# A gated gMLP and Mamba-2 layer on one core: the wide products gathered in three PSUM banks, and sums moved between GpSimd, VectorE and ScalarE

## The chip, the core and the metric

The kernel runs on one core of a Trainium2 chip: TensorE (PE) multiplies 128x128 tiles into PSUM, which has eight banks of 128x512 float32; VectorE (DVE), ScalarE (ACT) and GpSimd (POOL) do the elementwise work; DMA queues are fed by SyncE (SP) and ScalarE. Each engine takes its instructions in a fixed order. The metric is the time of one execution in microseconds (us), lower is better.

## The reference

One layer on a sequence of 1024 positions and 1024 channels, all in float32. Cut to what matters:

```python
h = rms_norm(x, norm_w) * (1 + scale) + shift                 # modulated by c
gm_u, gm_v, gm_z, ssm_z, xbc, dt_raw, g_a, g_b = split(h @ w_in)
y_a = gelu(gm_u) * (W_s @ layer_norm(gelu(gm_v)) + b_s) * silu(gm_z)     # chunks of 128
xs, bm, cm = split(silu(causal_conv(xbc, 4 taps)))
y_b = rms_norm((ssd_scan(xs, softplus(dt_raw), a, bm, cm) + xs * d_skip) * silu(ssm_z))
merged = sigmoid(g_a) * (y_a @ w_proj_a) + sigmoid(g_b) * (y_b @ w_proj_b)
return rms_norm(x + gate * (merged @ w_out))
```

`w_in` has 11296 columns. The product `h @ w_in` is most of the work.

## The kernel before

Float32 accuracy comes from splitting each operand into a high and a low part (`float32r`) and adding three products, high by high, high by low, low by high. Large products also go through a scheme of seven half-size products in place of eight (p1 to p7): sums of the quarters of both operands are taken first, and sums of the seven products afterwards.

**Start** (to about 77 us): norm and modulation of `x`, its sums `b11`, `t1` to `t4`, `b21`, `b22` and their splits, and the columns of `dt` and the first two gates in three accumulators of two banks each.

**Wide stage**: the other columns of `w_in` in 43 pairs of 128 columns (`todo`): four pairs of `gm_v` (`v0` to `v6`), eight that join a block of u and one of z (`uz`), sixteen for the convolution (`cb`, `x`), eight of `ssm_z` (`z`), seven of gates (`g`). For each pair:

- `pair_weights` loads four 128x512 pieces of `w_in` on SP's queue into a ring of eight slots (four pieces and three sums a pair, so the next pair's later pieces wait until slots come free), takes four sums of them (lines 526 to 529, on GpSimd; on VectorE for the first pair), and splits seven operands: a ScalarE copy for the high part (line 489), a VectorE subtraction for the low one (line 490). It is called one pair ahead; the split operands lie in rings of eight.
- `pair` runs the seven products (`product`, line 537, twelve matmuls each) and empties their banks. It takes five of the eight PSUM banks, `a b e c d`, in the order p1(a) p6(b) p7(e) p5(c) p4(d) p2(a again) p3(c again). `a` is copied by ScalarE (lines 550, 573); five sums from PSUM are VectorE's (lines 554, 560, 564, 568, 576). Both halves of an output row, `c1` and `c2`, build on each other in SBUF. An emptying has high priority in the scheduler that fixes each engine's order.
- What follows a pair (`d1`, `d2`): gelu and transposition for v; the convolution, one ScalarE pass, three VectorE passes (line 830) and a silu (line 832) per 128 channels; tanh for gates; for `uz`, sigmoid and products (lines 812 to 820). `mix_load` brings the block's LayerNorm input `vm` back and applies mean and scale in eight VectorE passes of 128 columns (line 791); `mix` multiplies it.
- `later` hangs tasks on slots, one a product: the mix, the weights of `w_proj_b` brought into split form quarter by quarter (`wb_quarter`, lines 735 to 755, from pair 22 on), `w_out` times the gate on GpSimd (line 718).

**After it**: the scan over chunks (two groups of heads in turn; `front`, `back`, `prep`, with the product by `w_proj_a` drawn in between by `draw`), then the product by `w_proj_b` and the one by `w_out`. The scan takes its PSUM tiles from the same eight banks through `bank`.

## Time and profile before

| | |
|---|---|
| median of 3 runs (lowest, highest) | 1453.49 us (1453.35, 1453.54) |
| the profiled execution: time, span, mean clock of TensorE | 1452.97 us, 1451.2 us, 0.993 |
| busy: PE, DVE, ACT, POOL | 97%, 78%, 49%, 33% of the span |

The time of an execution is a little over the span from first to last instruction in its trace. A row of a timeline has start, duration, engine, line, operation, output <- inputs, and in brackets the idle time of the engine before it with what ended it. A row of the waits has who waited for whom, then total, number and longest in us. A row of a group has its number of instructions after x, then busy time and the mean duration of one in ns. Line numbers in rows are those of the kernel they come from.

### The profile page before, as it was taken

The page shows a single profiled execution, that of the slowest core. Times are in us where ns is not written, and L with a number is a line of the kernel's source. Part 1 is how long each engine was busy: PE and PEld are TensorE (multiplying, and loading weights), DVE is VectorE, ACT ScalarE, POOL GpSimd, SP SyncE. Part 2 cuts the span into 40 slices and gives each one's busy share as a digit, 9 for nine tenths or more (in the row PEclk, how much of TensorE's full clock was granted, in tenths as well). Part 3 has the DMA queues.
Part 4 walks back from the last instruction along what each step waited for, and adds up shares of the span by engine and source line. Part 5 has one row for each costly group of instructions (what it writes and reads, how often), then busy time and mean ns, then how long its engine had stood idle before and what let it go on. Part 6 is the DMA issues. An engine that isn't in the chain of part 4 may idle for free.

```text
span 1451.2 us, 20751 instructions
## 1 busy us (share of the span) xinstructions
PE 1405.2 (97%) x7095; PEld 1158.3 (80%) x7095; DVE 1131.7 (78%) x1793; ACT 707.0 (49%) x1284; POOL 480.3 (33%) x366
## 2 busy tenths in 40 slices
PE   8989999999999999899989999999999999999997
PEld 6768888888888788778877888888878878787886
DVE  4676599999999998798999988588777667948443
ACT  5654454544445454444536544478776624334211
POOL 0032124233333233323342433147878840000000
PEclk9999999999999999999999999999999999999999
DMA  8543333323333564778657685598887767977331
GB/s 270 151 129 102 117 95 116 108 83 93 102 117 116 149 190 148 235 215 252 203 168 236 213 263 174 163 314 304 314 291 243 262 199 272 369 250 283 134 116 73
DMA packets 260461, 276.82 MB, mean 191 GB/s; under 512 B 13596, under 2 KB 210628, under 8 KB 260356
## 3 DMA queue, kind: packets, MB, share of 16 engines
q1 hardware_dynamic: 179364, 195.24, 42.6%
q10 hardware_dynamic: 80992, 80.26, 16.6%
q8 instruction: 56, 0.92, 0.3%
q14 instruction: 49, 0.40, 0.1%
HBM read 191.27 MB, written 84.18 MB: 190 GB/s over the span
## 4 chain that ended last, share of the span: by engine, by line
PE 33%; DMA 6%; DVE 5%; issue 3%; POOL 3%; ACT 2%; SPq 1%; POOLq 0%; ACTq 0%; DVEq 0%
PE po L76 6%; PE yp L1386 3%; PE x L1386 3%; PE pma L76 2%; DMA yn<-yb_d 2%; PE cz L537 2%; PE cg L537 1%; PE az L537 1%; PE ag L537 1%; PE yi L76 1%; PE yn L76 1%; DMA dcy<-acs_d 1%; DMA wol<-wo_d 1%; PE sp L76 1%; PE ccb L537 1%
## 5 line engine op out<-in xcount | busy, mean ns | idle before, releaser
L1582 POOL TENSOR_TENSOR r<-r,fnw 128x256 f32<-128x256 f32 (+1 forms) x3 | 2.7, 915 | 253.6 <-ACT xr L1581 253.6
L923 ACT ACTIVATE dcy<-dcy,nacs 128x128 f32<-128x128 f32 x256 | 78.2, 388 | 14.0 <-POOL dcy L918 13.9
L526 POOL TENSOR_TENSOR s1uz<-a21uz,a22uz 128x512 f32<-128x512 f32 x8 | 10.5, 1307 | 143.7 <-DMA a22uz<-in_w_in_dram 107.5
L918 POOL TENSOR_SCALAR_AFFINE_SELECT dcy<-dcy 128x1024 f32<-128x1024 f32 x32 | 35.4, 1108 | 41.7 <-ACT ea L915 41.6
L915 ACT ACTIVATE ea<-dcy 64x512 f32<-64x512 f32 x64 | 40.1, 626 | 17.3 <-DMA dcy<-acs_d 13.1
L832 ACT ACTIVATE ac<-ac 128x1024 f32<-128x1024 f32 x32 | 34.0, 1062 | 26.1 <-DVE ac L830 26.0
L830 DVE SCALAR_TENSOR_TENSOR ac<-c2cb,cwt,ac 128x1023 f32<-128x1023 f32 (+2 forms) x24 | 44.2, 1843 | 0.5 <-issue 0.2
L943 DVE TENSOR_TENSOR dcy<-dcy,pc 128x1024 f32<-128x1024 f32 x32 | 38.9, 1215 | 6.8 <-PE pc L79 5.1
L76 PE MATMUL pma<-yh,wah 128*128 128x512 f32 x128 | 43.4, 419 | 0.1
L971 POOL TENSOR_TENSOR st<-st,cd 128x256 f32<-128x256 f32 x48 | 34.5, 721 | 26.9 <-DVE st L969 16.6
L76 PE MATMUL pma<-yh,wal 128*128 128x512 f32 x128 | 42.7, 415 | 0.0
L1005 POOL TENSOR_TENSOR yz<-y,sl 128x512 f32<-128x512 f32 x32 | 42.3, 1322 | 0.9
L1004 POOL TENSOR_TENSOR y<-y,ym 128x512 f32<-128x512 f32 (+1 forms) x32 | 37.0, 1157 | 13.8 <-DVE ym L1003 13.2
L830 DVE SCALAR_TENSOR_TENSOR ac<-c2x,cwt,ac 128x1023 f32<-128x1023 f32 (+2 forms) x24 | 40.2, 1677 | 1.5 <-ACT ac L828 1.3
L1591 DVE TENSOR_TENSOR r<-po,xr 128x1024 f32<-128x1024 f32 x7 | 8.6, 1225 | 41.1 <-PE po L76 41.1
L791 DVE TENSOR_SCALAR vm<-vm,mv,vr 128x128 f32<-128x128 f32 x64 | 40.6, 704 | 0.0
L1592 ACT ACTIVATE xr<-r 128x1024 f32<-128x1024 f32 x7 | 7.4, 1061 | 67.3 <-issue 39.7
L1003 DVE TENSOR_TENSOR ym<-yn,ea 128x512 f32<-128x512 f32 (+1 forms) x32 | 19.9, 621 | 26.0 <-PE yn L76 25.9
L76 PE MATMUL pma<-yl,wah 128*128 128x512 f32 x128 | 40.1, 394 | 0.0
L526 POOL TENSOR_TENSOR s1x<-a21x,a22x 128x512 f32<-128x512 f32 x8 | 12.3, 1535 | 75.8 <-DMA a22x<-in_w_in_dram 19.3
L76 PEld LDWEIGHTS yn<-sl,st 128*128 128x128 f32 x224 | 30.7, 193 | 8.2 <-issue 2.4
L76 PE MATMUL yn<-sl,st 128*128 128x128 f32 x224 | 32.0, 279 | 4.7 <-DVE st L973 4.0
(2812 smaller groups left out, 4708.2 us busy)
## 6 DMA issues: line engine op xcount, KB each, us to landing
sl<-s_d SPq DMA_DIRECT2D x32, 768.0 KB, 6.1
s_d<-ac ACTq DMA_DIRECT2D x32, 512.0 KB, 3.2
dcy<-acs_d SPq DMA_DIRECT2D x32, 512.0 KB, 8.5
aw<-in_ada_w_dram SPq DMA_DIRECT2D x16, 512.0 KB, 3.9
wbr<-in_w_proj_b_dram SPq DMA_DIRECT2D x64, 128.0 KB, 3.9
wb_d<-wbb ACTq DMA_DIRECT2D x32, 256.0 KB, 3.4
wb_d<-wbc ACTq DMA_DIRECT2D x32, 256.0 KB, 3.2
yb_d<-yz ACTq DMA_DIRECT2D x32, 256.0 KB, 6.1
```

The costliest lines, as they stand in the source:

```text
L76: pin(PE.matmul(acc, l, r, start=first, stop=last))
L537: pin(PE.matmul(ps, lw[:, k * P : (k + 1) * P], r[k], start=first and n + k == 0, stop=n == 2 and k == 3, skip_group_check=not first))
L791: V.tensor_scalar(vn[:, cs], vn[:, cs], mv[:, ch, 0:1], vr[:, 1, ch : ch + 1], op0=ALU.subtract, op1=ALU.mult)
L830: V.scalar_tensor_tensor(ac[:, s:], cc[:, : S - s], conv_wt[:, 3 - s, i : i + 1], ac[:, s:], op0=ALU.mult, op1=ALU.add)
L915: A.activation(ea[hh * HD : (hh + 1) * HD], dcy.rearrange("p (j e) i l -> p e j (i l)", e=2)[hh * HD : (hh + 1) * HD, hh], AF.Exp)
L918: G.affine_select(out=d8, in_=d8, compare_op=ALU.is_ge, fill=-1e30, base=0, pattern=[[0, 2 * HPG], [1, P]], channel_multiplier=-1)
L923: A.activation(dcy[:, h, i, :], dcy[:, h, i, :], AF.Exp, bias=sub[:, i, h : h + 1])
L943: V.tensor_tensor(d3, d3, pc[:, 0:256].unsqueeze(1).to_broadcast([P, HPG, 256]), op=ALU.mult)
L971: G.tensor_mul(v3(s2), v3(self.st), fac(cd, g, s)[:, i].unsqueeze(2).to_broadcast([P, HPG, HD]))
L1004: G.tensor_add(y1[:, :, t0:], y1[:, :, t0:], m[:, :, t0:])
L1005: G.tensor_mul(yz, y1, sl[:, 4:6])
L1386: pin(PE.matmul(ps[j], a[:, v, js], r, start=first and n + k == 0, stop=n == 2 and k == KT - 1, skip_group_check=not first))
```

## The change

Seven products with other banks and in another order; four weight sums and one product from GpSimd to VectorE; the LayerNorm factor from VectorE to ScalarE; sigmoid as one silu on ScalarE; another order of the last pairs.

TensorE. A pair has three banks: x (its own ring of two) gathers p1, then p6, p7 and p4 on top; y gathers p5 and p3; z has p2. x is read out after each product without being cleared. p4 runs in the next pair, after its p5, except where a pair is `whole` (pairs `v6`, `z7` and the last), which ends with p7, p2, p4. One row for each product (four matmuls have it alike but for the tile of k; the rest is left out), in the pair `cb2` before:

```order
L537 MATMUL acb_3121<-b11h_155,p1cb2h 128x512
...
L537 MATMUL bcb_3122<-t2h_163,p6cb2h 128x512
...
L537 MATMUL ecb_3123<-t3h_171,p7cb2h 128x512
...
L537 MATMUL ccb_3124<-t1h_179,p5cb2h 128x512
...
L537 MATMUL dcb_3125<-t4h_187,p4cb2h 128x512
...
L537 MATMUL acb_3121<-b21h_195,p2cb2h 128x512
...
L537 MATMUL ccb_3124<-b22h_203,p3cb2h 128x512
```

and now, with the first products of the pair `uz4`:

```order
L560 MATMUL xcb_3086<-b11h_155,p1cb2h 128x512
...
L560 MATMUL ycb_3101<-t1h_163,p5cb2h 128x512
...
L560 MATMUL xcb_3086<-t2h_171,p6cb2h 128x512
...
L560 MATMUL ycb_3101<-b22h_179,p3cb2h 128x512
...
L560 MATMUL zcb_3158<-b21h_195,p2cb2h 128x512
...
L560 MATMUL xcb_3086<-t3h_187,p7cb2h 128x512
...
L560 MATMUL xuz_3236<-b11h_155,p1uz4h 128x512
...
L560 MATMUL yuz_3264<-t1h_163,p5uz4h 128x512
...
L560 MATMUL xcb_3086<-t4h_203,p4cb2h 128x512
```

Between two products of one bank there are now two others.

ScalarE, at the end of the pair `uz3` and the start of `cb2` (`c1uz` holds the block's u before and its z now, `tz` the tanh for its sigmoid, `p1uz4h` a high part for the pair after), before:

```order
L812 ACTIVATE tz_3035<-c2uz_2995 128x1024
L489 CAST p3cb2h<-s4cb_2917 128x512
L573 COPY c1uz_2980<-auz_2950 128x512
L489 CAST p1uz4h<-a11uz_3078 128x512
L819 ACT_TABLE_LOAD
L819 ACTIVATE c1uz_2980<-c1uz_2980 128x1024
L550 COPY c1cb_3138<-acb_3121 128x512
```

and now:

```order
L576 COPY c1uz_2940<-xuz_2914 128x512
L840 ACTIVATE vm_3031<-vm_3031,vr 128x128 x8
L508 CAST p2cb2h<-a12cb_2877 128x512
L878 ACTIVATE ac_2970<-ac_2970 128x1024
L508 CAST p7cb2h<-a21cb_2873 128x512
L88 DMA s_d_118<-ac_2970 512x1x256
L859 ACTIVATE c1uz_2940<-c1uz_2940 128x1024
L508 CAST p4cb2h<-a22cb_2875 128x512
L508 CAST p1uz4h<-a11uz_3043 128x512
L576 COPY c1cb_3099<-xcb_3086 128x512
```

The eight passes of the LayerNorm factor came in; the first copy of `cb2` no longer has the gelu with its table load just ahead of it.

VectorE at the same place, before:

```order
L814 SCALAR_TENSOR_TENSOR ya_2967<-c2uz_2995,ya_2967 128x1024
L791 TENSOR_SCALAR vm_3064<-vm_3064,mv,vr 128x128 x8
L576 TENSOR_TENSOR c1uz_2980<-c1uz_2980,cuz_2953 128x512
L490 TENSOR_TENSOR p1uz4l<-a11uz_3078,p1uz4h 128x512
L490 TENSOR_TENSOR p6uz4l<-s2uz_3087,p6uz4h 128x512
L554 TENSOR_TENSOR c1cb_3138<-c1cb_3138,bcb_3122 128x512
```

and now, from the p7 addition of the pair `x1` to the p3 addition of `uz3` (two splits and one convolution pass are left out):

```order
L576 TENSOR_TENSOR c2x_2869<-p5x_2792,xx_2764 128x512
L509 TENSOR_TENSOR p4uz3l<-a22uz_2725,p4uz3h 128x512
L876 SCALAR_TENSOR_TENSOR ac_2850<-c1x_2777,cwt,ac_2850 128x1022
...
L876 SCALAR_TENSOR_TENSOR ac_2850<-c1x_2777,cwt,ac_2850 128x1021
L851 SCALAR_TENSOR_TENSOR ya_2927<-mix_0_2928,par_140,bsb 128x512
L851 SCALAR_TENSOR_TENSOR ya_2927<-mix_1_2934,par_140,bsb 128x512
L509 TENSOR_TENSOR p5cb2l<-s1cb_2879,p5cb2h 128x512
L509 TENSOR_TENSOR p6cb2l<-s2cb_2880,p6cb2h 128x512
L876 SCALAR_TENSOR_TENSOR ac_2970<-c2x_2869,cwt,ac_2970 128x1023
...
L876 SCALAR_TENSOR_TENSOR ac_2970<-c2x_2869,cwt,ac_2970 128x1021
L576 TENSOR_TENSOR c1uz_2940<-c1uz_2940,yuz_2942 128x512
```

The factor's block is gone from VectorE. The diff, cut to its core:

```diff
     hpool = tc.tile_pool(name="hpool", bufs=1, reuse_waits="tile")
     hp = hpool.__enter__()
-    BN = ("b11", "t2", "t3", "t1", "t4", "b21", "b22")
+    BN = ("b11", "t1", "t2", "b22", "t3", "b21", "t4")
...
-            pin(A.activation(sg[:, h * 512 : (h + 1) * 512], accs[i][h], AF.Tanh, scale=0.5))
-        store(th_d[(i - 1) * P : i * P, :], sg)
+            A.activation(sg[:, h * 512 : (h + 1) * 512], accs[i][h], AF.Tanh, scale=0.5)
+        later(1 + i, store, th_d[(i - 1) * P : i * P, :], sg)
     def first_dt():
         dtt = wide("dtt")[0:NH, :]
         for h in range(2):
             pin(V.tensor_copy(dtt[:, h * 512 : (h + 1) * 512], accs[0][h][0:NH, :]))
-        store(dt_d, dtt)
+        later(2, store, dt_d, dtt)
...
     def bank(name):
-        return psum.tile([P, 512], F32, name=name, tag="bk", bufs=8)
+        if pairs_done:
+            pairs_done.append(name)
+            if len(pairs_done) % 4 == 2:
+                return psum.tile([P, 512], F32, name=name, tag="px", bufs=2)
+        return psum.tile([P, 512], F32, name=name, tag="bk", bufs=6)
...
-    def split(name, t, keep):
-        hi, lo = wt(f"{name}h", "wh", 8), wt(f"{name}l", "wl", 8)
-        keep(A.copy(hi, t))
-        keep(V.tensor_sub(lo, t, f32(hi)))
-        return hi, lo
-    def pair_weights(name, c1, c2, pinned=False):
+    def pair_weights(name, c1, c2, pinned=False, parts_later=False):
...
         s1, s2, s4 = (wt(f"s{i}{name}", "ws", 8, F32) for i in (1, 2, 4))
         s3 = a["21"]
-        parts = {"p1": a["11"], "p6": s2, "p7": s3, "p5": s1, "p4": a["22"], "p2": a["12"], "p3": s4}
+        parts = {"p1": a["11"], "p5": s1, "p6": s2, "p3": s4, "p2": a["12"], "p7": s3, "p4": a["22"]}
         ops = {}
         def parts_of(*nms):
             for nm in nms:
-                ops[nm] = split(f"{nm}{name}", parts[nm], pin if pinned else lambda i: i)
+                if nm not in ops:
+                    ops[nm] = wt(f"{nm}{name}h", "wh", 8), wt(f"{nm}{name}l", "wl", 8)
+                (hi, lo), t, keep = ops[nm], parts[nm], pin if pinned or parts_later else lambda i: i
+                keep(A.copy(hi, t))
+                keep(V.tensor_sub(lo, t, f32(hi)))
         if pinned:
+            for nm in parts:
+                ops[nm] = wt(f"{nm}{name}h", "wh", 8), wt(f"{nm}{name}l", "wl", 8)
+            parts_of("p1")
+            pin(V.tensor_add(s1, s3, a["22"]))
+            first_dt()
+            parts_of("p5")
+            pin(V.tensor_sub(s2, s1, a["11"]))
+            last_split("t2")
+            parts_of("p6")
+            first_gate(1)
+            first_gate(2)
+            def stage(n):
+                if n == 0:
+                    pin(V.tensor_sub(s4, a["12"], s2))
+                    parts_of("p3")
+                elif n == 1:
+                    parts_of("p2")
+                    pin(V.tensor_sub(s3, a["11"], s3))
+                    last_split("t3")
+                elif n == 2:
+                    parts_of("p7")
+                    last_split("t4")
+                    parts_of("p4")
+                    seconds.extend(pair_weights(*todo[1][:3], parts_later=True))
+                elif n == 3:
+                    seconds[1]("p1")
+                elif n == 4:
+                    seconds[1]("p5", "p6")
+                elif n == 5:
+                    seconds[1]("p3", "p2", "p7", "p4")
+            ops["after"] = stage
+        else:
             V.tensor_add(s1, s3, a["22"])
             V.tensor_sub(s2, s1, a["11"])
...
-        else:
-            G.tensor_add(s1, s3, a["22"])
-            G.tensor_sub(s2, s1, a["11"])
-            G.tensor_sub(s3, a["11"], s3)
-            G.tensor_sub(s4, a["12"], s2)
-            parts_of("p1", "p6", "p7", "p5", "p4", "p2", "p3")
+            V.tensor_sub(s4, a["12"], s2)
+            V.tensor_sub(s3, a["11"], s3)
+            if parts_later:
+                return ops, parts_of
+            parts_of("p1", "p5", "p6", "p3", "p2", "p7", "p4")
         return ops
...
-    def pair(name, ops, done2, done1, after=None):
-        keep = pin if after else lambda i: i
+    pending, pairs_done = [], []
+    def pair(name, ops, done1, done2, after=None, whole=False):
+        keep = pin if name in first_c1 and not p2r else lambda i: i
         after = after or (lambda n: None)
-        pa, pb, pe, pc, pd = (bank(f"{n}{name}") for n in "abecd")
-        product(pa, ops["p1"], "b11")
-        c1 = wide(f"c1{name}")
-        u2 = c1[:, 512:1024]
-        with tc.high_priority():
-            keep(A.copy(u2, pa))
+        def out(f, *a):
+            with tc.high_priority():
+                keep(f(*a))
+        def p2():
+            pz = bank(f"z{name}")
+            product(pz, ops["p2"], "b21")
+            out(V.tensor_add, c1[:, 0:512], c1[:, 0:512], pz)
+        px = psum.tile([P, 512], F32, name=f"x{name}", tag="px", bufs=2)
+        product(px, ops["p1"], "b11")
+        c1 = first_c1.pop(name) if name in first_c1 else wide(f"c1{name}")
+        out(A.copy, c1[:, 0:512], px)
         after(0)
-        product(pb, ops["p6"], "t2")
-        with tc.high_priority():
-            keep(V.tensor_add(u2, u2, pb))
+        py = bank(f"y{name}")
+        product(py, ops["p5"], "t1")
+        c2 = wide(f"c2{name}") if p2r else None
+        p5 = c2[:, 512:1024] if p2r else gm.tile([P, 512], F32, name=f"p5{name}", tag="p5")
+        out(A.copy, p5, py)
         after(1)
-        c2 = wide(f"c2{name}")
-        product(pe, ops["p7"], "t3")
-        u3 = c2[:, 0:512]
-        with tc.high_priority():
-            keep(V.tensor_add(u3, u2, pe))
+        if pending:
+            pending.pop()()
+        product(px, ops["p6"], "t2", False)
+        out(A.copy, c1[:, 512:1024], px)
         after(2)
-        product(pc, ops["p5"], "t1")
-        with tc.high_priority():
-            keep(V.tensor_add(c2[:, 512:1024], u3, pc))
+        product(py, ops["p3"], "b22", False)
+        out(V.tensor_add, c1[:, 512:1024], c1[:, 512:1024], py)
         after(3)
-        product(pd, ops["p4"], "t4")
-        with tc.high_priority():
-            keep(V.tensor_add(u3, u3, pd))
-        after(4)
-        done2(c2)
-        product(pa, ops["p2"], "b21", False)
-        with tc.high_priority():
-            keep(A.copy(c1[:, 0:512], pa))
-        product(pc, ops["p3"], "b22", False)
-        with tc.high_priority():
-            keep(V.tensor_add(u2, u2, pc))
-        done1(c1)
+        if not whole:
+            p2()
+            after(4)
+            done1(c1)
+        product(px, ops["p7"], "t3", False)
+        c2 = c2 or wide(f"c2{name}")
+        out(V.tensor_add, c2[:, 512:1024], p5, px)
+        after(4 if whole else 5)
+        if whole:
+            p2()
+            done1(c1)
+        def p4():
+            product(px, ops["p4"], "t4", False)
+            out(A.copy, c2[:, 0:512], px)
+            done2(c2)
+        if whole:
+            p4()
+        else:
+            pending.append(p4)
...
-    wst = gx.tile([P, NG, P], F32, name="wst", tag="wst")
+    first_c1 = {"v0": gx.tile([P, S], F32, name="c1v0", tag="wst")}
+    wst = None
...
         rsqrt(vr[:, 1, :], vr[:, 0, :], vr[:, 2, :])
+        V.scalar_tensor_tensor(vr[:, 2, :], mv[:, :, 0], -1.0, vr[:, 1, :], op0=ALU.mult, op1=ALU.mult)
...
-            V.tensor_scalar(vn[:, cs], vn[:, cs], mv[:, ch, 0:1], vr[:, 1, ch : ch + 1],
-                            op0=ALU.subtract, op1=ALU.mult)
+            A.activation(vn[:, cs], vn[:, cs], AF.Identity, scale=vr[:, 1, ch : ch + 1], bias=vr[:, 2, ch : ch + 1])
...
     def zg_done(g):
         def done(cz):
-            th = wide(f"tz{g}")
-            A.activation(th, cz, AF.Tanh, scale=0.5)
-            V.scalar_tensor_tensor(cz, th, 1.0, cz, op0=ALU.add, op1=ALU.mult)
-            V.scalar_tensor_tensor(vns[g], cz, 0.5, vns[g], op0=ALU.mult, op1=ALU.mult)
+            A.activation(cz, cz, AF.Silu)
+            V.tensor_mul(vns[g], cz, vns[g])
         return done
     def u_done(g):
         def done(cu):
             A.activation(cu, cu, AF.Gelu_apprx_tanh)
-            G.tensor_mul(cu, cu, vns[g])
+            V.tensor_mul(cu, cu, vns[g])
...
-        jobs.append((f"uz{g}", COL_U + g * P, COL_ZG + g * P, u_done(g), zg_done(g), g))
+        jobs.append((f"uz{g}", COL_ZG + g * P, COL_U + g * P, zg_done(g), u_done(g), g))
     light = [p for q in zip(light, gpairs[:5] + [None] * 3) for p in q if p]
-    n_l = len(light)
-    while convs or light:
-        if convs:
-            jobs.append(convs.pop(0))
-        take = 2 if len(light) > len(convs) else 1
-        for _ in range(take if convs or len(light) < 3 else len(light)):
-            if light:
-                jobs.append(light.pop(0))
+    while convs:
+        jobs.append(convs.pop(0))
+        for _ in range(1 if len(convs) in (1, 4, 7) else 2):
+            jobs.append(light.pop(0))
...
-            later(3, decays, n + 1)
+            later(3 + 5 * n, decays, n + 1)
             g, s = order[n]
-            later(12 + n, groups[g].prep, s)
+            later(13 + n, groups[g].prep, s)
...
-    held = []
-    NPRE = 22
+    held, seconds = [], []
+    NPRE = 20
...
-                later(2 + 4 * i, wb_quarter, i)
+                later(2 + 43 * i // 10, wb_quarter, i)
...
-        if n + 1 < len(todo):
+            first_c1[name] = wide(f"c1{name}")
+        if 0 < n < len(todo) - 1:
             nxt = pair_weights(*todo[n + 1][:3])
...
-            later(1, mix, g)
+            later(1 if g else 3, mix, g)
             if g + 1 < NG:
                 later(7, mix_load, g + 1)
         if n + 1 == len(todo):
-            pair(name, ops, lambda t: held.append((d2, t)), lambda t: held.append((d1, t)), beside)
+            pair(name, ops, lambda t: held.append((d1, t)), lambda t: held.append((d2, t)), beside, True)
         else:
-            pair(name, ops, d2, d1)
-        ops = nxt
+            pair(name, ops, d1, d2, ops.get("after"), n in (3, len(jobs) - 1))
+        ops = nxt if n else seconds[0]
...
+    pairs_done.append("")
...
+    draw(6)
     for n in range(2):
         step(n, "front")
         draw(10)
```

More of the change, by code (lines that the diff above doesn't have):

```diff
@@ L633, in dt_part1d @@
         V.tensor_scalar_mul(dthq, dth, 2.0)
-        later(4, dt_part2, dth, adt)
+        later(8, dt_part2, dth, adt)
     def dt_part2(dth, adt):
@@ L669, in mix_weights2 @@
     def mix_weights2(wsn):
+        nonlocal wst
+        wst = gx.tile([P, NG, P], F32, name="wst", tag="wst")
         for q in range(2):
```

13 lines of the change are left out of this document (removed).

## Prediction

> **What bounds the kernel now.** I read the engine shares first, then the table by stage, then TensorE's waits, then the timelines around the longest of them.
>
> ```profile
> PE 1405.2 (97%) x7095; PEld 1158.3 (80%) x7095; DVE 1131.7 (78%) x1793; ACT 707.0 (49%) x1284; POOL 480.3 (33%) x366
> ...
> 77.00:490.00 413.00, 406.48 (x1879) 336.62 (x1878) 350.63 (x496) 196.21 (x279) 140.33 (x91) 1.00 0.36 110
> 490.00:800.00 310.00, 296.30 (x1287) 241.68 (x1286) 278.20 (x413) 151.10 (x257) 108.41 (x66) 0.98 0.68 203
> 800.00:956.00 156.00, 156.00 (x700) 129.40 (x698) 122.32 (x172) 80.98 (x141) 48.59 (x32) 1.00 0.68 213
> ```
>
> The columns of the lower rows are the stretch and its length, then busy time of TensorE, its weight loads, VectorE, ScalarE and GpSimd, then the clock. The wide stage is 77 to 956 us, 43 column pairs; then comes the scan. TensorE sets the time, so only its idle time and a lowered clock can be won. VectorE is its only rival: 350.63+278.20+122.32 = 751 of the wide stage's 879 us.
>
> ```profile
> PE cz L537 <- DVE c2z L564: 8.0, 4, 3.5
> PE cg L537 <- DVE c2g L564: 5.2, 2, 4.3
> PE cv L537 <- DVE c2v L564: 4.8, 1, 4.8
> ...
> PE cuz L537 <- DVE c2uz L564: 1.7, 1, 1.7
> ...
> PE cx L537 <- DVE c2x L564: 0.5, 1, 0.5
> ```
>
> All waits of the wide products have one form: p3 wants bank `c` again, two products after p5 left it (p4 and p2 lie between), and VectorE has not yet made the addition of line 564 that empties it. They sum to 8.0+5.2+4.8+1.7+0.5 = **20.2 us**. The three longest also lower the clock:
>
> ```profile
> 99.33 2.08 PE L537 MATMUL cv<-b22h,p3v0h 128*128 128x512 f32 x4 [4.77 <-DVE c2v L564]
> ...
> 103.49 1.07 PE L537 MATMUL av<-b11h,p1v2h 128*128 128x512 f32 x4
> ...
> 732.07 2.08 PE L537 MATMUL cg<-b22h,p3g8h 128*128 128x512 f32 x4 [4.30 <-DVE c2g L564]
> 737.22 1.09 PE L537 MATMUL acb<-b11h,p1cb6h 128*128 128x512 f32 x4
> 739.97 1.07 PE L537 MATMUL bcb<-t2h,p6cb6h 128*128 128x512 f32 x4
> 742.69 1.07 PE L537 MATMUL ecb<-t3h,p7cb6h 128*128 128x512 f32 x4
> ...
> 778.10 2.08 PE L537 MATMUL cz<-b22h,p3z4h 128*128 128x512 f32 x4 [3.51 <-DVE c2z L564]
> 782.48 1.08 PE L537 MATMUL ag<-b11h,p1g10h 128*128 128x512 f32 x4
> ```
>
> An undisturbed product of twelve matmuls takes 742.69-739.97 = 2.72 us. After the three waits it took 103.49-99.33 = 4.16, 737.22-732.07 = 5.15 and 782.48-778.10 = 4.38: 1.44+2.43+1.66 = **5.5 us** more. So 25.7 us of the wide stage hang on VectorE being late.
>
> **Why VectorE is late.** Two things, both touched by the change.
>
> ```profile
> 89.41 1.79 DVE L490 TENSOR_TENSOR p2v0l<-a12v,p2v0h 128x512 fp32r<-128x512 f32 x1
> ...
> 96.20 0.67 DVE L554 TENSOR_TENSOR c1v<-c1v,bv 128x512 f32<-128x512 f32 x1
> 96.79 0.68 DVE L490 TENSOR_TENSOR p7v2l<-a21v,p7v2h 128x512 fp32r<-128x512 f32 x1
> ```
>
> ```profile
> 90.72 1.63 POOL L527 TENSOR_TENSOR s2v<-s1v,a11v 128x512 f32<-128x512 f32 x1
> ```
>
> While GpSimd sums weights, VectorE's subtraction of two SBUF tiles takes 1.79 us; alone 0.68. Undisturbed operations of this size follow each other at 0.60 (96.20 to 96.79). An addition out of PSUM keeps 0.67. Over the wide stage the split's subtractions (line 490), the convolution (830) and the LayerNorm factor (791) hold VectorE this long:
>
> ```profile
> 77.00:956.00 879.00, 260.71 (x301) 0.99 0.53 161
> 77.00:956.00 879.00, 145.26 (x96) 0.99 0.53 161
> 77.00:956.00 879.00, 40.56 (x64) 0.99 0.53 161
> ```
>
> 301 at 0.60 would be 181, so 80 us of the first are GpSimd's doing; the convolution's are 1.27 us when undisturbed (row `c1cb` below), 96 x 1.2 = 115 from start to start, so 30 of the second. And a block in the queue makes others late:
>
> ```profile
> 330.02 6.18 DVE L791 TENSOR_SCALAR vm<-vm,mv,vr 128x128 f32<-128x128 f32 x8
> 332.07 1.07 PE L537 MATMUL acb<-b11h,p1cb2l 128*128 128x512 f32 x4
> 336.12 0.68 DVE L576 TENSOR_TENSOR c1uz<-c1uz,cuz 128x512 f32<-128x512 f32 x1
> 336.88 1.28 ACT L819 ACT_TABLE_LOAD   x1 [6.71 <-DVE c1uz L576]
> 339.14 0.57 ACT L550 COPY c1cb<-acb 128x512 f32<-128x512 f32 x1
> ```
>
> Product p1 of `cb2` ended at 333.1; ScalarE copied it 6.0 us later, because it stood behind a gelu that waited for VectorE, which was 6.18 us in line 791.
>
> **The change, part by part.** TensorE's products are as many and as long as before (the same matmuls in another order), so nothing there.
>
> VectorE loses two PSUM additions a pair (86 x 0.60 = 52 us), line 791 (41 us), and the 110 us of GpSimd's disturbance; gains four weight sums in 42 pairs (168 x 0.60 = 101 us) and the product with u. The gates are priced by
>
> ```profile
> L830 DVE SCALAR_TENSOR_TENSOR ac<-c1cb,cwt,ac 128x1023 f32<-128x1023 f32 x8 | 10.2, 1272 | 0.2 <-ACT ac L828 0.2
> L814 DVE SCALAR_TENSOR_TENSOR ya<-c2uz,ya 128x1024 f32<-128x1024 f32 x8 | 10.8, 1354 | 0.0
> L813 DVE SCALAR_TENSOR_TENSOR c2uz<-tz,c2uz 128x1024 f32<-128x1024 f32 x8 | 9.8, 1225 | 3.8 <-ACT tz L812 3.7
> L923 ACT ACTIVATE dcy<-dcy,nacs 128x128 f32<-128x128 f32 x16 | 4.9, 389 | 2.4 <-POOL dcy L918 2.4
> ```
>
> two passes before (9.8+10.8), two multiplications after (16 x 1.2): nothing. Sum: 751-52-41-110+101-1 = 648 us, 76% of a stage of some 855. GpSimd keeps eight multiplications of `w_out`; if each disturbs two operations by 1.79-0.68, the bound from above is 666. ScalarE gains 86 copies at 0.57 and 64 factors; I price these by the nearest row, line 923, 0.39: 428+49+25 = 502 us, 59%. Neither engine is a bound on average.
>
> The banks. Each pair now holds x (p1, p6, p7, p4), y (p5, p3) and z (p2), and every bank is wanted again after two products: 2 x 2.72 = **5.44 us** for an evacuation, where before only `c` had so little. The copy of `acb` above, done 6.6 us after its product, would miss that. What made it late goes: in the new order there stand between ScalarE's copy of p6 in the pair before and this copy the factor's eight passes, two Silus and four casts. With
>
> ```profile
> L832 ACT ACTIVATE ac<-ac 128x1024 f32<-128x1024 f32 x32 | 34.0, 1062 | 26.1 <-DVE ac L830 26.0
> L489 ACT CAST p3cb0h<-s4cb 128x512 fp32r<-128x512 f32 x1 | 0.6, 627 | 0.1
> ```
>
> that is 8 x 0.39+2 x 1.06+4 x 0.63 = 7.8 us of work in the time of four products, 10.9 us. On VectorE, from the p7 addition of a conv pair to the p3 addition of the next stand five operations of 0.60, five of the convolution at 1.2 and two of the mix that are no dearer, 11.4 us, in five products, 13.6 us. So both queues have room. Six places have only one product between uses, 2.72 us: p1 to p6 where no p4 is held over (`v0`, `cb0`, `g12`), and p7 to p4 in the three pairs kept whole. I take 0.5 us for each, 3 us; the bounds are 0 (ScalarE idle, copy 0.57) and 6 x 2.7 = 16.
>
> The first pair's 4.77 us came from VectorE being in weight splits of `v2` at 1.78 us when five products waited for emptying; now GpSimd is silent, the splits come in the products' order, and each product of `v0` is emptied behind it. It is in the 25.7.
>
> Loads. The same loads in the same order stand on SP's queue, but a22 and a12 of the next pair now take slots that p7 and p4 leave, the sixth and seventh split instead of the third and fifth. Behind them on SP wait the `vm` and `wbr` loads.
>
> ```profile
> a22x<-in_w_in_dram SPq DMA_DIRECT2D x8, 256.0 KB, 5.0
> ```
>
> 5.0 us to landing and 0.60 for the sum, against three products (8.2 us) from p7's split to p5's of the next pair: hidden. It would cost up to 3 us a pair only if the splits ran less than two products ahead.
>
> The scan stage pays. The eight banks are split six and two there too, with every fourth tile from the two. Where each tile's bank comes from is fixed in the built program: before, only one bank is refilled less than 1.4 us of matmuls after its last product; now nine are, the shortest being `pc1_1`, which takes the bank of `px0_1` with one transposed state product between. Emptying such a bank takes
>
> ```profile
> 1019.34 0.38 PE L79 MATMUL px<-ident,sl 128*128 128x128 f32 x2
> ...
> 1019.59 1.22 DVE L943 TENSOR_TENSOR dcy<-dcy,pc 128x1024 f32<-128x1024 f32 x1 [0.52 <-PE pc L79]
> ...
> 1021.33 0.68 DVE L939 TENSOR_TENSOR xe<-px,dde 128x512 f32<-128x512 f32 x1
> ```
>
> 2.3 us from the last transpose to the end of `xe` (`xd`, as long, comes between), 1.1 less without line 943 first. Four of the nine are `px` banks, at 0.2, 0.9, 0.9 and 0.9 us: 2.3 to 6.3 us of waiting; the others are `yn` banks, emptied by one operation in about 0.7 us. I take 4 us. Six steps of the next projection's products are drawn before the first front and may hide a wait there; I count nothing.
>
> **Sum.** The profiled execution took 1452.97 us (span 1451.2), 0.5 below the median. 1452.97-25.7+3+4 = 1434.3: **1434 us**.
>
> The Trainium skill speaks against three banks: "TensorE: Matmul & The Clock Gate", section "A second HAM failure mode: psum-queue depth-cycling", has a kernel that cycles through PSUM banks idle so often that the clock swings to half and back. Its rule would put a price of its own on short waits (rival 1); that page counts an idle window of about 3.4 us before the clock falls. Right after a wait of 3.1 us (one of the four on `cz`) the clock, the last column but two, stays at 1.00, and the three waits above 3.4 us are those that cost 5.5 us; the trace agrees with the window:
>
> ```profile
> 588.00:590.00 2.00, 1.66 (x7) 1.40 (x8) 1.94 (x3) 0.00 (x0) 0.00 (x0) 1.00 0.95 283
> ```
>
> **Rivals.**
> 1. *The banks are too few (slower).* If ScalarE's copies stay as late as that of `acb`, 6.57 us after the product, each pair waits 6.57-5.44 = 1.13 us at one bank: 43 x 1.13 = 49, in place of the 3: 1480 us. It decides from a mean overrun of 0.5 us a pair (22/43). For it: both queues are in order and carry more cross-waits. Against it: the cause of that lateness leaves VectorE. If such waits also lowered the clock for one product a pair, 5.15 for 2.72, it would be 43 x 2.4 = 105 us dearer.
> 2. *Half.* VectorE at 76% still falls behind where the projection's weight quarters crowd it (490 to 800, 278 of 310 us now); half of the 15.4 us of waits there and their clock stay: 1434+10 = 1444.
> 3. *The scan hides all*: its bank waits fall where VectorE is early anyway, and the one-product places cost nothing: 1452.97-25.7 = 1427. Against it: TensorE is the busy engine there too, and 0.2 us is less than any way of emptying.
> 4. *It moves and does not shrink*: VectorE's lag becomes ScalarE's, 1453.
>
> **How the numbers follow.** The forecast 0.60 (1428 to 1442: with the six places at 0 and the scan at 2.3 it is 1429.6, with 9 of the possible 16 us at the six places and the scan at 6.3 it is 1442), rival 2 0.14, rival 3 0.11, rival 4 0.05, rival 1 0.10. The first, second and third are faster: 0.85; the fourth 0.05 within 0.2% (2.9 us, about what can be told from no change); slower 0.10. The range takes in the first three, with 3 us below the third for waits too short to be listed and the forecast's full 16 us above: 1423 to 1450.
>
> **What would show it.** Right: TensorE's waits on the wide products under 5 us in sum, the clock 1.00 through the stage, line 509's mean near 680 ns, VectorE near 650 us there, and the stage shorter by some 23 us; new waits of `pc` and `sp` on `xe` in the scan, some 4 us. Wrong: x or y products waiting for ScalarE copies pair after pair; VectorE above 720 us; or the scan more than 8 us longer.

## The result, and the profile after

| | before | after |
|---|---|---|
| median (lowest, highest), four executions each | 1453.51 us (1453.35, 1457.92) | 1433.03 us (1429.22, 1434.62) |
| ratio after to before, 95% interval | | 0.9848 (0.9821 to 0.9875) |
| profiled execution: span | 1451.2 us | 1431.4 us |

One of six executions of the kernel `nod` below took 4393.9 us, three times the others, and is left out everywhere.

Forecast: 1434. The total was nearly exact, but two of its terms were wrong by 7 us each, in opposite directions: that it fits is luck. The wide stage is counted from its first product to the end of its last, the scan from there to the first product of the last stages, here in TensorE's timeline of the kernel before and of the one after:

```profile
77.18 1.07 PE L537 MATMUL av<-b11h,p1v0h 128*128 128x512 f32 x4
...
955.24 1.08 PE L537 MATMUL cg<-b22h,p3g14l 128*128 128x512 f32 x4
...
1192.36 0.39 PE L1386 MATMUL x<-p1bh,p1a 128*128 128x512 f32 x1
```

```profile
76.19 1.07 PE L560 MATMUL xv<-b11h,p1v0h 128*128 128x512 f32 x4
...
924.24 1.08 PE L560 MATMUL xg<-t4h,p4g14l 128*128 128x512 f32 x4
...
1175.14 0.39 PE L1431 MATMUL x<-p1bh,p1a 128*128 128x512 f32 x1
```

The ends of the wide stage are 955.24+1.08 = 956.32 and 924.24+1.08 = 925.32. It went from 879.1 to 849.1 us, **30.0 shorter** (forecast: 25.7-3 = 22.7). The scan went from 236.0 to 249.8, **13.8 longer** (forecast: 4). What stands behind the scan went from 258.9 to 256.3, and the start is 1.0 shorter. So behind the wide products the change loses 13.8-2.6 = 11.2 us. The stage table of the kernel after, with the columns of the prediction's:

```profile
PE 1401.6 (98%) x7095; PEld 1161.5 (81%) x7095; DVE 1026.6 (72%) x1812; ACT 783.2 (55%) x1436; POOL 204.4 (14%) x190
...
76.00:925.00 849.00, 849.00 (x3852) 703.95 (x3851) 645.92 (x1100) 506.95 (x833) 23.43 (x11) 1.00 0.55 166
...
925.00:1060.00 135.00, 128.46 (x939) 110.92 (x938) 102.80 (x181) 94.14 (x243) 93.54 (x92) 0.97 0.83 285
1060.00:1190.00 130.00, 120.67 (x804) 103.35 (x805) 88.27 (x160) 67.27 (x163) 81.55 (x74) 0.96 0.68 234
```

In the wide stage TensorE is busy all the time at full clock, VectorE 645.92 us (76%). The splits of line 509 and the convolution take, in two more answers of that view:

```profile
76.00:925.00 849.00, 213.98 (x301) 1.00 0.55 166
```

```profile
76.00:925.00 849.00, 122.63 (x96) 1.00 0.55 166
```

In the scan the clock of TensorE is now 0.97 and 0.96. Before it was 0.99 and 1.00:

```profile
956.00:1090.00 134.00, 129.51 (x964) 111.82 (x963) 108.06 (x191) 101.95 (x261) 102.40 (x98) 0.99 0.87 303
1090.00:1215.00 125.00, 120.80 (x804) 102.94 (x803) 87.03 (x159) 63.82 (x152) 74.73 (x69) 1.00 0.67 223
```

The two longest of TensorE's listed waits in the scan, before:

```profile
PE yn L76 <- DVE st L973: 4.0, 2, 2.2
...
PE pq L76 <- POOL sq L1024: 1.6, 1, 1.6
```

and all of them after:

```profile
PE pq L76 <- POOL sq L1066: 4.4, 1, 4.4
PE yn L76 <- DVE st L1015: 4.3, 3, 2.8
PE pc L76 <- issue: 1.9, 1, 1.9
PE sp L76 <- DVE ssq L1073: 1.7, 1, 1.7
PE sp L76 <- DVE xe L981: 1.2, 2, 0.6
PE yn L76 <- POOL yz L1066: 1.2, 1, 1.2
PE yi L76 <- DVE st L1015: 1.1, 1, 1.1
```

They sum to 15.8 us, against 8.5 before. The lowered clock, added up over windows of four microseconds, costs 8.5 us at four places instead of 1.7 at one. 15.8+8.5-8.5-1.7 = 14.1, about the scan's 13.8.

### The profile page after: what moved, and what is told of

Read it like the earlier page. It is cut to its first block, busy times and chain, and to the rows that moved or that the text cites. A ratio compares the mean times of both kernels' runs of the same rounds, so it can differ in the third digit from the quotient of the medians.

```text
span 1431.4 us, 20514 instructions
## 1 busy us (share of the span) xinstructions
PE 1401.6 (98%) x7095; PEld 1161.5 (81%) x7095; DVE 1026.6 (72%) x1812; ACT 783.2 (55%) x1436; POOL 204.4 (14%) x190
## 4 chain that ended last, share of the span: by engine, by line
PE 85%; DMA 6%; POOL 2%; issue 2%; DVE 2%; ACT 1%; SPq 1%; POOLq 0%; ACTq 0%; DVEq 0%
PE xcb L560 6%; PE xz L560 6%; PE xuz L560 6%; PE xx L560 6%; PE po L76 6%; PE xg L560 5%; PE x L1431 5%; PE pma L76 4%; PE yp L1431 3%; PE xv L560 3%; PE yuz L560 3%; PE ycb L560 3%; PE yx L560 3%; PE yz L560 3%; PE yg L560 3%
## 5 line engine op out<-in xcount | busy, mean ns | idle before, releaser
L766 POOL TENSOR_TENSOR wog<-wog,gb 128x1024 f32<-128x1024 f32 x8 | 20.1, 2517 | 723.6 <-DMA wbr<-in_w_proj_b_dram 549.0
L76 PE MATMUL sp<-xe,bn 128*128 128x256 f32 x112 | 34.5, 427 | 2.9 <-DVE ssq L1073 1.7
L76 PE MATMUL yi<-dcy,xd 128*64 128x128 f32 x512 | 35.9, 284 | 1.1 <-DVE st L1015 1.1
L876 DVE SCALAR_TENSOR_TENSOR ac<-c2x,cwt,ac 128x1023 f32<-128x1023 f32 (+2 forms) x24 | 30.7, 1279 | 7.6 <-ACT ac L874 6.1
L876 DVE SCALAR_TENSOR_TENSOR ac<-c2cb,cwt,ac 128x1023 f32<-128x1023 f32 (+2 forms) x24 | 30.7, 1279 | 7.3 <-ACT ac L874 5.8
```

The costliest lines, as they stand in the source:

```text
L76: pin(PE.matmul(acc, l, r, start=first, stop=last))
L876: V.scalar_tensor_tensor(ac[:, s:], cc[:, : S - s], conv_wt[:, 3 - s, i : i + 1], ac[:, s:], op0=ALU.mult, op1=ALU.add)
```

## The experiments

The columns wide, scan and behind (what stands behind the scan) are in us, from TensorE's timelines as above; the ratio is to the kernel before in the same comparison, and its interval is 0.002 to 0.003 to either side. Stages are those of one profiled execution each, which can lie some us off the median (`scan8` 1439.7 against 1434.6, `nod` 1433.4 against 1437.0): a few us in one stage may be that execution.

| kernel | median | ratio | wide | scan | behind |
|---|---|---|---|---|---|
| before | 1453.5 to 1456.4 | 1 | 879.1 | 236.0 | 258.9 |
| after | 1433.0 | 0.9848 | 849.1 | 249.8 | 256.3 |
| scan8 | 1434.6 | 0.9855 | 851.7 | 252.1 | 256.9 |
| nod | 1437.0 | 0.9869 | 849.7 | 247.8 | 257.2 |
| scan8nod | 1437.7 | 0.9865 | 849.9 | 250.7 | 258.8 |
| scanold | 1438.9 | 0.9885 | 851.2 | 247.6 | 261.3 |
| powlate | 1429.7 | 0.9836 | 849.1 | 240.3 | 263.6 |
| b4draw6 | 1460.1 | 1.0044 | 880.9 | 245.6 | 256.5 |
| b4ssd | 1464.6 | 1.0067 | 880.0 | 244.7 | 262.2 |
| whole | 1442.9 | 0.9912 | 859.9 | 247.4 | 256.8 |
| sumsG | 1466.0 | 1.0075 | 883.8 | 247.9 | 256.5 |
| b4sumsV | 1439.5 | 0.9888 | 862.6 | 240.0 | 258.4 |
| light22 | 1439.6 | 0.9897 | 856.5 | 247.1 | 257.2 |
| factorV | 1431.5 | 0.9847 | 849.1 | 246.3 | 257.4 |

The first question was the scan's 13.8 us, in three kernels made from the change.

**scan8**, eight banks in one ring again:

```diff
-            pairs_done.append(name)
-            if len(pairs_done) % 4 == 2:
-                return psum.tile([P, 512], F32, name=name, tag="px", bufs=2)
+            return psum.tile([P, 512], F32, name=name, tag="bk", bufs=8)
...
     pairs_done.append("")
+    ps1.__exit__(None, None, None)
+    ps1 = tc.tile_pool(name="ps1s", bufs=1, space=PSUM, reuse_waits="tile")
+    psum = ps1.__enter__()
```

> The changed kernel, but with its eight banks in one ring again from the scan on; TensorE's order is untouched. After the change the scan takes 249.8 us (925.3 to 1175.1) where it took 236.1: 13.7 more, not 4. Theory (two causes): the split of the banks costs 8 us of this, namely the waits of pc at 946 (1.9, and 1.7 of lowered clock around it), of sp at 992 and 1107 (0.6 each) and of sp at 1136 (1.7, and 1.7 of lowered clock), so those four go, the scan takes about 242 and the run about 1425; the wait of 4.4 us on the GpSimd sum of squares at 1167 stays. Rival (banks alone): all 13.7 go, the run is near 1420. Rival (neither: the scan merely begins 31 us sooner and outruns its loads): the waits move, the run stays within 2 us of 1433.

**nod**, without the steps ahead:

```diff
-    draw(6)
     for n in range(2):
         step(n, "front")
```

> The changed kernel without the six steps of the projection that are drawn ahead of the first front; banks split six and two as in the change. Theory (two causes): the six steps taken ahead are missing at the scan's end, where VectorE's order then has the last sums of squares behind a row that waits for a load; without them the wait at 1167 (4.4 us, and 3.4 of lowered clock after it) falls to what it was before, 1.6 us without loss of clock, so 6 us less there; some 2 us of it may be lost again in front of the scan, where the steps covered a wait: 1427 to 1429. Rival (banks alone): no change at the end, 1433 or up to 3 us more, because the first bank waits lose their cover. Rival (neither): within 2 us of 1433.

**scan8nod** has both edits.

> Both: one ring of eight banks in the scan and no steps of the projection ahead of the first front, so the scan is emitted as in the kernel before. Theory (two causes): the scan takes again 236 to 238 us, the wide stage stays at 849 us: 1419 to 1421. Rival (banks alone): the same as with the ring of eight, no more. Rival (neither): within 3 us of 1433, with the scan still near 250 us.

Measured: 252.1, 247.8 and 250.7 us of scan, and no median below the change's. Both theories on banks fall: with eight banks the wait of `pc` and those of `sp` on `xe` were gone, and others of the same size stood elsewhere. Of `nod` one part came true, at the end of the scan. VectorE's timeline there, after:

```profile
1162.77 0.75 DVE L1370 SCALAR_TENSOR_TENSOR yn<-yn,par,rb 128x512 f32<-128x512 f32 x1 [2.34 <-DMA yn<-yb_d]
1163.44 0.15 DVE L1073 TENSOR_SCALAR ssq<-pq 128x4 f32<-128x4 f32 x1
```

and GpSimd's:

```profile
1163.68 2.02 POOL L1077 TENSOR_TENSOR ssq<-ssq,nhalf 128x8 f32<-128x8 f32 x1 [6.39 <-DVE ssq L1073]
1165.67 1.51 POOL L1066 TENSOR_TENSOR sq<-sq,sq 128x512 f32<-128x512 f32 x1
```

The small `ssq` stands behind a row that waits for a load; GpSimd's power waits for it, and behind the power stands the sum for which TensorE then waits 4.42 us. Without `draw(6)` VectorE's order had `ssq` first again and the wait was 1.77 us. But the scan was only 2 us shorter in the profile, and the median, if anything, higher.

**powlate**: on GpSimd the sum goes ahead of that power.

```diff
-                G.tensor_tensor(ssq[:, c8], ssq[:, c8], nhalf, op=ALU.pow)
+                if g == NG - 1:
+                    c16 = ssq[:, (g - 1) * NCH : (g + 1) * NCH].rearrange("p (a b) -> p a b", a=2)
+                    G.tensor_tensor(c16, c16, nhalf.unsqueeze(1).to_broadcast([P, 2, NCH]), op=ALU.pow)
+                elif g != NG - 2:
+                    G.tensor_tensor(ssq[:, c8], ssq[:, c8], nhalf, op=ALU.pow)
```

> The changed kernel with one edit at the scan's end: GpSimd's power for the last but one group is done together with that of the last group, so that on GpSimd the last sum of squares no longer stands behind a power that waits for VectorE (row ssq of line 1073, itself behind a row of line 1370 that waits 2.34 us for its load). TensorE's and SP's orders stay as they were. Theory (one blocked queue): ScalarE's squares end at 1162.0, the sum can be done by 1163.4, so the wait at 1167 falls from 4.4 to about 1 us, and the 3.4 us of lowered clock behind it go too: the scan takes 243 us instead of 250, the run 6 to 7 us less than 1433: about 1426. Rival (given back): the last stage's first products then wait for their operands, whose rows of line 1370 wait for the same loads, and the run stays at 1431 to 1434.

TensorE's waits in this kernel, from the end of the wide products to 1175 us:

```profile
PE x L1435 <- DVE tha L1268: 2.1, 1, 2.1
PE pc L76 <- issue: 1.9, 1, 1.9
PE sp L76 <- DVE ssq L1073: 1.8, 1, 1.8
...
PE pq L76 <- POOL sq L1066: 0.7, 1, 0.7
```

The wait fell to 0.7 and the scan to 240.3 us, 9.5 shorter. The edit explains about 7 of these: 3.7 of the wait and 3.4 of the clock behind it. Another 3.4 us of clock were not lost at two places that the edit does not touch, the waits of `pc` and `sp` above (last section). But the products behind it took 263.6, 7.3 longer: they waited for their operands (4.8 us of waits instead of 0.9) and the clock fell twice more. The rival is right for most of it: given back. Against the change the gain is not measurable (0.981 to 0.9861 beside 0.9821 to 0.9875).

**scanold** undoes the last of the scan's edits too:

```diff
-            later(3 + 5 * n, decays, n + 1)
+            later(3, decays, n + 1)
             g, s = order[n]
-            later(13 + n, groups[g].prep, s)
+            later(12 + n, groups[g].prep, s)
```

> The changed kernel with all of the scan's own edits undone: one ring of eight banks, no six steps ahead, and the decays and the two first preps due at the slots of before, so that VectorE has the multiplications of both preps ahead of most splits of the projection's operand again. Theory (late preps: in the change VectorE ends the second prep 8 us after the last wide product, before 0.5 us ahead of it, and the fixed order never makes it good): the scan takes 236 to 240 us, the run 1420 to 1424. Rival (redrawn order: TensorE's order in the scan is fixed ahead by estimated times, and any edit gives another set of places where it waits): the scan stays at 246 to 253, with waits at other places, the run within 4 us of 1435.

247.6 us: late preps are not it either. All the scan's edits undone, the run is slower than the change, if anything. (Compared row by row by name, TensorE's order in this scan is nearly that of before again, those of VectorE, ScalarE and GpSimd less so.) So the same edits were put into the kernel before, whose wide stage stays: **b4draw6** has `draw(6)` ahead of the first front, **b4ssd** the two due slots (the diff just shown, the other way round).

> The kernel before with one thing of the change: six steps of the projection drawn ahead of the first front. Wide stage as before. What stands behind the wide products (scan, last stages) took 494.9 us before, 504 to 510 in the change and in nine kernels made from it, 498.4 with only the sums moved. Theory (favourable order): TensorE's order there is written ahead by estimated times, that of before happens to fit, and any redrawing costs 5 to 15 us: here 500 to 510 behind the wide products, with the wait for the last sum of squares at 4 us as in the change (VectorE's order has the load's row ahead of it again), the run 1459 to 1468. Rival (the three-bank wide stage leaves something late): 493 to 499, the run within 4 us of 1455.

> The kernel before with only the due slots of the first decays and preps as in the change (the second decays five slots later, the preps one). Theory (favourable order): as above, 499 to 508 us behind the wide products, at least 4 more than before, the run 1458 to 1466; the last sum of squares keeps its wait of 1.6 us. Rival (the three-bank wide stage leaves something late): 493 to 498, the run within 3 us of 1455.

The wide stage stayed at 881 and 880 us; what stands behind it took 502.1 and 506.9 us, against 494.9. The medians moved by 6.6 and 11.1 us. In `b4draw6` the wait for the last sum of squares is 4.2 us, the 4 that were expected: `draw(6)` brings it in this kernel too. TensorE's longest waits in `b4ssd`, those of the wide products and of the start left out:

```profile
PE yn L76 <- DVE st L973: 7.0, 5, 1.7
...
PE yi L76 <- issue: 2.9, 1, 2.9
PE x L1386 <- DVE tha L1221: 2.6, 1, 2.6
PE pq L76 <- POOL sq L1024: 1.7, 1, 1.7
```

That fits the theory of the favourable order, with one correction. An edit that neither adds nor removes work costs 7 to 12 us by the order alone, which each queue then keeps whatever happens; but it is hardly TensorE's order that is redrawn. By name (buffer numbers left out), 99% of TensorE's rows of the scan in `b4ssd` and all of SyncE's stand in the order of before, and only 87, 72 and 67% of VectorE's, GpSimd's and ScalarE's. TensorE's waits are for these three, but for one of 2.9 us with no releaser.

The other question was what the 30 us of the wide stage consist of.

**b4sumsV**, the kernel before with its weight sums on VectorE:

```diff
-            G.tensor_add(s1, s3, a["22"])
-            G.tensor_sub(s2, s1, a["11"])
-            G.tensor_sub(s3, a["11"], s3)
-            G.tensor_sub(s4, a["12"], s2)
+            V.tensor_add(s1, s3, a["22"])
+            V.tensor_sub(s2, s1, a["11"])
+            V.tensor_sub(s3, a["11"], s3)
+            V.tensor_sub(s4, a["12"], s2)
```

> The kernel before with one thing of the change: the four weight sums of every pair on VectorE in place of GpSimd. VectorE's work in the wide stage is about the same (751 - 110 + 101 = 742 us), but none of it comes in bunches of 1.79 us. Theory (contention made the lateness): the waits of the wide products for the emptying of bank c fall from 20.2 us to under 6, the wide stage from 879 to 855 to 860, the run to about 1432. Rival (the block of line 791 and the number of additions made it): waits stay above 12 us, the stage above 868, the run above 1443. For the scan, whose code is that of before: if its order of rows were by itself what made it 236 us, it stays within 4 us of that; if 236 was one draw of an order that any change redraws, it comes out elsewhere, as the four others did at 248 to 252.

```profile
PE cv L537 <- DVE c2v L564: 5.2, 1, 5.2
...
PE cz L537 <- DVE c2z L564: 1.7, 2, 1.5
...
PE mix L76 <- DVE vm L791: 1.4, 1, 1.4
```

16.5 us of the 30 come with this edit alone, a little less than expected (862.6 us for 855 to 860, a median of 1439.5 for 1432). VectorE is as full as before (723.96 us of the stage's 863), but the waits on bank `c` are 6.9 us instead of 20.2. 5.2 of them are the first pair's, whose sums were VectorE's already; with the clock that falls there (3.4 us by windows) it makes 8.6 of the missing 13.5. GpSimd is silent during that wait, so in the first pair it is VectorE's own splits and sums that are in the way. Everywhere else contention, not load, made VectorE late. The scan, in nearly the order of before, took 240.0 us.

**sumsG**, the change with the sums from the third pair on back on GpSimd:

```diff
-            V.tensor_add(s1, s3, a["22"])
-            V.tensor_sub(s2, s1, a["11"])
-            V.tensor_sub(s4, a["12"], s2)
-            V.tensor_sub(s3, a["11"], s3)
+            E = V if parts_later else G
+            E.tensor_add(s1, s3, a["22"])
+            E.tensor_sub(s2, s1, a["11"])
+            E.tensor_sub(s4, a["12"], s2)
+            E.tensor_sub(s3, a["11"], s3)
```

> The changed kernel with the weight sums of the 41 pairs from the third on back on GpSimd; banks and order of the products as in the change. VectorE gives up 164 sums (98 us) and gets GpSimd's disturbance back (in the trace before 110 us, in bunches of operations of 1.79 us). Theory (the banks' order carries the gain, contention only adds): evacuations come up to 2 us later where a bunch falls on them, waits of 3 to 12 us in the wide stage, 1436 to 1447. Rival (contention was the whole cause): the 20 us of waits and 5 of clock come back, 1455 or more. Rival (contention is harmless once two products stand between uses): within 2 us of 1433.

The first rival came true (1455 or more): the wide stage took 883.8 us, 34.7 more than the change and 4.7 more than before, with 23.3 us of listed waits for x and y banks and 6.8 of lowered clock. Rows of VectorE's timeline ahead of the longest wait, and that wait on TensorE:

```profile
667.81 2.07 DVE L877 SCALAR_TENSOR_TENSOR ac<-c1x,cwt,ac 128x1023 f32<-128x1023 f32 x1 [0.17 <-ACT ac L875]
669.80 2.55 DVE L789 TENSOR_TENSOR wbc<-wbr,wbc 128x256 fp32r<-128x256 f32 x1
672.28 0.68 DVE L577 TENSOR_TENSOR c2x<-p5x,xx 128x512 f32<-128x512 f32 x1
```

```profile
673.01 1.20 PE L561 MATMUL xx<-t4h,p4x5h 128*128 128x512 f32 x4 [3.37 <-DVE c2x L577]
```

Two SBUF operations of 2.07 and 2.55 us, one beside a sum on GpSimd, one beside its `w_out` product (which the change keeps there), and the x bank is 3.37 us late for p4. With GpSimd at work three banks are no better than five; they need it quiet.

**whole**, one product between all uses of x and y:

```diff
-            pair(name, ops, d1, d2, ops.get("after"), n in (3, len(jobs) - 1))
+            pair(name, ops, d1, d2, ops.get("after"), n > 0)
```

> The changed kernel with every pair from the second on kept whole: p4 ends its own pair and is not held over, so one product (2.72 us) stands between all uses of the x bank and of the y bank, where the change has two. Theory (spacing): in the trace of the change 36 of 172 emptyings of p1, p5, p6 and p7 are done later than 2.72 us after their product, 36.7 us of lateness in sum; with that spacing TensorE waits 20 to 37 us for them, more where a wait lowers the clock: the wide stage takes 870 to 890 us instead of 849, the run 1455 to 1475. By the price of the prediction (0.5 us at each such place, four a pair) it would be 80 us: 1515. Rival (the queues were the cause and the spacing is spare): an emptying that is waited for is merely done sooner, waits under 6 us, the run within 4 us of 1433.

859.9 us, 10.8 more, waits of 7.3, no fall of the clock. Below both prices for spacing, above the rival: some 170 such places cost 0.06 us each on average. With GpSimd quiet the spacing is worth a third of the wide stage's gain, not all of it.

**light22** puts the old order of the light pairs back (the loop over `convs` and `light` of the diff), and `wb_quarter` with it:

```diff
-    NPRE = 20
+    NPRE = 22
-                later(2 + 43 * i // 10, wb_quarter, i)
+                later(2 + 4 * i, wb_quarter, i)
```

> The changed kernel with the light pairs in the order of before (the gates and z pairs in twos, x7 third from last) and the quarters of w_proj_b from pair 22 on, one every four products, as before. Theory (the order carries part of the gain): where z and g pairs stand next to each other between 560 and 800 us VectorE and ScalarE are late again, waits of 5 to 12 us with one or two falls of the clock, the wide stage 856 to 864 instead of 849, the run about 1443. Rival (with two products between uses the order is worth nothing): the stage within 3 us of 849. For the scan: if the order of the last pairs is what made it 250 us, it comes back to 236 to 241 here; if not, it stays at 246 to 252.

```profile
892.09 1.07 PE L560 MATMUL yg<-t1h,p5g12l 128*128 128x512 f32 x4
896.97 2.07 PE L560 MATMUL xg<-t2h,p6g12h 128*128 128x512 f32 x4 [3.81 <-ACT c1g L576]
900.54 1.91 PE L560 MATMUL xg<-t2h,p6g12l 128*128 128x512 f32 x4
```

856.5 us, 7.4 more, by one wait and the half clock behind it, at one of the six places that the prediction named: p1 to p6 of `g12`, where no p4 is held over. In ScalarE's queue two silus of the convolution `x7` stood ahead of the copy, both waiting for VectorE; in the change the pair ahead is `z7`. Between 560 and 800 us, where I had expected it, the order was worth nothing.

**factorV**, the LayerNorm factor on VectorE:

```diff
-            A.activation(vn[:, cs], vn[:, cs], AF.Identity, scale=vr[:, 1, ch : ch + 1], bias=vr[:, 2, ch : ch + 1])
+            V.tensor_scalar(vn[:, cs], vn[:, cs], mv[:, ch, 0:1], vr[:, 1, ch : ch + 1],
+                            op0=ALU.subtract, op1=ALU.mult)
```

> The changed kernel with the LayerNorm factor back on VectorE (64 operations of some 0.63 us, about 40 us, in blocks of two and six), off ScalarE (64 of 0.483, 31 us). Theory (room): VectorE has 849 - 700 us free in the stage and the blocks are now split by a convolution pass, so an addition behind a block of six is 3.8 us later, which stays under the 5.44 us that two products give: waits under 3 us, the run within 3 us of 1433. Rival (the block was a cause): in each of the eight pairs an evacuation misses its bank by 1 to 2 us: the stage 857 to 865, the run about 1445.

849.1 us, no wait: the move was worth nothing. The groups of this operation in the kernel before, here, and on ScalarE in the change:

```profile
L791 DVE TENSOR_SCALAR vm<-vm,mv,vr 128x128 f32<-128x128 f32 x64 | 40.6, 704 | 0.0
```

```profile
L840 DVE TENSOR_SCALAR vm<-vm,mv,vr 128x128 f32<-128x128 f32 x64 | 17.7, 341 | 0.0
```

```profile
L840 ACT ACTIVATE vm<-vm,vr 128x128 f32<-128x128 f32 x64 | 25.6, 483 | 1.2 <-DMA vm<-v_d 1.2
```

23 of the 41 us that I took for the factor were GpSimd's doing as well: in `b4sumsV`, which moves nothing but the sums, the 64 operations of line 791 hold VectorE 17.1 us.

## Why the prediction was right or wrong

- **The wide stage's waits and clock (-25.7): right in cause, too small.** None of the 20.2 us is left. For the first pair the cause was incomplete: `b4sumsV` has GpSimd silent there and still waits 5.2 us, and only the change, with its splits in the order of the products, is rid of it; that order was not tried alone. The clock was mis-sized: I counted the product behind each of three waits, 5.5; windows over the stage give 6.9. The last 2.9 of the 30.0 stand in no listed wait and no clock window; where they lie is not shown, and I had put nothing for them.
- **The six places with one product (+3): nothing, and there are twelve.** Between p5 and p3 of `v0`, `cb0` and `g12`, and between p6 and p7 of the three pairs kept whole, stands one product too: in `v0` p5 starts at 78.91, p6 at 81.70 and p3 at 84.42. No listed wait stands at any of them. A price per place was the wrong form: some 170 of them cost 10.8 us, and one of them 7.4, by what stands ahead in ScalarE's queue.
- **The scan (+4): the step that failed, 13.8 in its place, 11.2 with what stands behind it.** The predicted waits came (`pc` 1.9, `sp` on `xe` 1.2; the profile names no releaser for `pc`, and that it is the bank of `px0_1` is inferred), yet eight banks did not shorten the scan. I priced a few bank distances as if the rest of its order stood still. Nine kernels made from the change take 504 to 510 us behind the wide products, two made from before by an edit of that order alone 502 and 507, `b4sumsV` 498, before 495. That redrawing is enough is shown; whether the three-bank stage adds a few us of its own is open, and a little of before's 495 may be that one execution (its later medians lie up to 3 us higher).
- **VectorE 648, ScalarE 502 us: 646 and 507.** VectorE's sum fits by luck, with terms mis-sized inside that cancel. Splits and convolution, counted at 110 us of disturbance, gave back 47 (260.71 to 213.98) and 23 (145.26 to 122.63); I had taken 0.60 us for the undisturbed operation, the step from start to start, against rows that count from start to end. And the quarters of `w_proj_b` (lines 740 and 752 to 755, now 788 and 800 to 803), which I did not count, gave back 45 (122.3 to 77.2 us of busy time). ScalarE's factor came to 25.6 us of busy time, for 25: a pass lasts 0.483 us from start to end, not line 923's 0.39, but the passes of a block overlap.
- **Room for evacuations (5.44 us): true, and thin.** The latest emptying of an x bank that p4 wants back, p7 of `z5`, ended on VectorE 5.2 us after its product:

```profile
825.13 1.07 PE L560 MATMUL xz<-t3h,p7z5l 128*128 128x512 f32 x4
```

```profile
830.68 0.68 DVE L576 TENSOR_TENSOR c2z<-p5z,xz 128x512 f32<-128x512 f32 x1
```

- **GpSimd's disturbance decided.** With it the change is slower than before (`sumsG`, ratio 1.0075), which is rival 1 on VectorE's side. I had priced its end as room on VectorE (76%); what counted is that its bunches went, since `b4sumsV` gains 16.5 us at 84%. Operations from SBUF to SBUF grow beside GpSimd, line 791's from 341 to 704 ns on average. Additions out of PSUM do not. The row at 96.20 in the prediction does not show that, since GpSimd's last sum ended at 95.7; their sums in the wide stage do, 87.63 us with GpSimd at work (`sumsG`) and 87.83 without (the change). The Trainium skill, "SBUF — State Buffer", section "SBUF: two separate sides", calls the port pair of GpSimd and VectorE an exclusive lock that blocks the loser for a whole instruction, against a VectorE operation in a two-port mode or with two SBUF inputs; these runs agree (additions out of PSUM have one SBUF input):

```profile
76.00:960.00 884.00, 87.63 (x129) 99.86 (x171) 0.99 0.53 160
```

```profile
76.00:925.00 849.00, 87.83 (x129) 99.92 (x171) 1.00 0.55 166
```

- **Signs.** Waits of wide products gone, clock 1.00, VectorE at 646: right. Line 509's mean was 0.71 us (213.98 over 301), a little above 0.68. The sign against ("the scan more than 8 us longer") came true as well: a total that fits does not show that its terms do. The stage was 30.0 us shorter, not some 23.

## What to carry to other kernels

Before fewer buffers are given more turns, look for what makes the emptying engine late in bunches: here an engine at the same load cost 16.5 us less once another stopped working beside it, and three banks without that were no better than five. A stage whose order is written ahead by estimated times has a price of its own for any edit that touches it: in this kernel the nine made from the change, the change and two made from before came out 7 to 15 us dearer there, so put a range of that size on it and try the edit on the old kernel alone. A spare place is priced by what can stand ahead in the emptying engine's queue, not by its number.
